# T4 of the last value pair grown by accumulating transfers, T1 of the first pair summed in DRAM

## The chip, the cores and the metric

The kernel runs on one core of a Trainium2 chip. The metric is the device time of one execution in microseconds; the median of three runs is taken. TensorE (PE in the profile) multiplies, VectorE (DVE), ScalarE (ACT) and GpSimd (POOL) work element by element, and the queues of SyncE (SP) and GpSimd issue transfers.

## What is computed

Two decoder layers on a sequence of 512 rows of 2048 numbers. Each layer has one input projection, three groups of attention heads, a gate, an output projection and a LayerNorm. Cut to what matters here:

```python
h = x @ w_in                    # 512 x 2048 by 2048 x 8278
fq, fk, fv, fg, ..., mq, mg = split(h)
y_fox = fox_attention(fq, fk, fv, ...) * silu(fg)
y_dsa = dsa_attention(dq, dk, dv, ...) * silu(dg)
y_mem = memory_attention(mq, mem @ w_mem_kv) * silu(mg)
x = layer_norm(ALPHA * x + concat(y_fox, y_dsa, y_mem) @ w_out)
```

The change touches the part of `x @ w_in` that the kernel calls the value columns: queries and keys of four heads, and the values and gates of twelve, 4096 columns in all.

## The kernel before, in words

**Numbers in two parts.** Each float32 operand is split into a high part (`whi`, by ScalarE, L217) and a low part (`wlo`, by VectorE, which subtracts the high part, L218). A product is three matmuls (L224 to L226): high by high, high by low, low by high. VectorE's `wlo` comes after ScalarE's `whi`, and TensorE needs both: the second matmul of a half already reads `wlo`.

**Seven products in place of eight.** The value columns come in four pairs of 512-column blocks (pair 0 to 3). For each pair the weights form a 2 by 2 grid of blocks, and the activations too, and the Strassen-Winograd scheme makes the result with seven products (`PRODUCTS`). Four of them read weight blocks as they lie in DRAM or a sum of blocks:

- P7 reads T3 = block (0,1) + block (1,1), summed in DRAM long before.
- Q6 reads T2 = T3 + block (0,0). The buffer that held T3 is grown: after it has been split for P7, GpSimd's queue issues a transfer that adds block (0,0) to it in place (`grow_w`, L283).
- Q4 reads T4 = T2 + block (1,0). VectorE adds the raw block (1,0), which was loaded for P2, to the buffer of T2 (`make_w`, L293). Until then the raw buffers of both are held.
- Q5 reads T1 = block (0,0) + block (0,1). SyncE loads one block into a raw buffer (L258) and the other into two slots (`other`, L264), and VectorE adds them (`pair_w`, L275).

**Order.** The order is written out by hand. A layer has the stages index, mem, values, heads and out, and a layer after the first begins with kv. In the stage values all pairs first run `VAL_FIRST` (P1, P7, P2, Q6 and Q4, mixed; its last chunks are Q6, Q6, P2, Q4, Q4), then all pairs run `VAL_SECOND` (Q5, Q5, Q3, Q3). So pair 3 of `VAL_FIRST` is followed by pair 0 of `VAL_SECOND`. Each name stands for two chunks (g = 0, 1). A chunk is 128 by 2048 numbers (1 MB) and is worked in two halves of 128 by 1024; a half feeds 12 matmuls of 512 columns. While half n is multiplied, half n+3 is split, half n+4 is summed by `pair_w`, and half n+2 starts to be grown. The split parts lie in four buffers each for `whi` and `wlo` (pool `whl`), so the split of half n+3 can only start once TensorE has left half n-1. The raw halves lie in six buffers (pool `raws`).

**What else VectorE does there.** In `VAL_FIRST` it builds the left operands S1 (for Q5) and S4 (for Q3) out of the activations (`val_operands`, L813, with the low parts in L823; the high parts are ScalarE's, L818), and it combines results on their way out of PSUM (`val_out`, L895 to L906). The results of Q5 and Q3 are copied out by ScalarE (L910). Q3 accumulates into the same two PSUM banks as Q5, so it can start only after that copy. The results go to DRAM by transfers on GpSimd's queue (`store_v`, L920 and L922).

**Sums in DRAM.** `all_sums` (L435) issues sums of weight blocks on GpSimd's queue: for each step of a sum a copy (L423) or an accumulating transfer (L404) of 1 MB from DRAM to DRAM. `paced` spreads the steps over the chunks, and outside the stage values each waits for a mark of VectorE (`pool_waits`, L391), so that GpSimd doesn't run ahead. In `weight_sums` T3 of the four value pairs of a layer takes 16 such transfers, which go out before that layer's values.

Of the kernel before, what the change touches and what calls it, by code (L numbers as in the profile page):

```python
# [80 lines left out]
PAIRS = 4  # L81
# [8 lines left out]
PAIRED = {"T1": ((0, 0), (0, 1))}  # L90
# [20 lines left out]
def all_chunks():  # L111

    out = []
    for l in range(DEPTH):
        out += [("mv", l, 0, g) for g in range(4)]
        out += [("mk", l, j, j * HD) for j in range(H_MEM)]
        out += layer_chunks(l)
    return out


def stream():

    wall = all_chunks()
    where = {c: i for i, c in enumerate(wall)}
    out = []

    def product(kind, l, name, pair, gs=(0, 1)):
        right = PRODUCTS[name][2]
        for g in gs:
            at = lambda step: where[kind, l, 2 * pair + step[1], 2 * step[0] + g]  # L130
            if kind == "val" and name in GROWN:
                of, step = GROWN[name]
                src = ("grown", (of, at(step)))
            elif kind == "val" and right in PAIRED:
                src = ("pair", tuple(at(step) for step in PAIRED[right]))
            elif isinstance(right, str):
                src = ("sum", (kind, l, right, pair, g))
            else:
                src = ("wall", at(right))
            out.append(({"val": "vs"}.get(kind, kind), l, (name, pair), g, src))  # L140

    for i, c in enumerate(wall):
        kind, l, j = c[:3]
        if kind == "out":
            if c == ("out", l, 0, 0):
                for name, pair in OUT_ORDER:
                    product("out", l, name, pair)
        elif kind == "val":
            if c == ("val", l, 0, 0):
                for order in (VAL_FIRST, VAL_SECOND):  # L150
                    for pair in range(PAIRS):
                        for name, g in order:
                            product("val", l, name, pair, (g,))
        else:
            out.append((*c, ("wall", i)))
    return out
# [20 lines left out]
def kernel(  # L177
# [25 lines left out]
    def uid(name):  # L203
        count[0] += 1
        return f"{name}_{count[0]}"
# [28 lines left out]
    for i, (kind, l, j, g, (how, key)) in enumerate(chunks):  # L234
        if how == "grown":
            of = place[kind, l, (key[0], j[1]), g]
            if j[0] == "Q6":
                grows[of] = i
            else:
                lender = place[kind, l, ("P2", j[1]), g]  # L240
                makes[max(of, lender)] = i
                lends[i] = (of, lender)
# [148 lines left out]
    def pool_waits():  # L391

        mark, seen = small("mark", 1), small("seen", 1)
        nc.vector.tensor_copy(mark, mhalf)  # L394
        nc.gpsimd.tensor_tensor(seen, mark, mhalf, op=ALU.mult)  # L395
# [4 lines left out]
    def block(kind, l, pair, g, step):  # L400
        return wall[where[kind, l, 2 * pair + step[1], 2 * step[0] + g]]

    def add_weights(key, src):
        nc.gpsimd.dma_start(sums[key], src, accum_op=ALU.add, max_dma_last_dim=4 * DM)  # L404

    def weight_sums(kind, l, names, pairs):

        for name in names:
            for n, step in enumerate(SUM_STEPS[name]):
                for pair in pairs:  # L410
                    for g in range(2):
                        key = (kind, l, name, pair, g)
                        if isinstance(step, str):
                            src = sums[kind, l, step, pair, g]
                        else:
                            src = block(kind, l, pair, g, step)
                        if now[1] != "values":
                            pool_waits()
                        if n:
                            add_weights(key, src)  # L420
                        else:
                            sums[key] = dram.tile([P, DM], F32, name=uid("sum"))
                            nc.gpsimd.dma_start(sums[key], src)  # L423
                        yield

    def paced(gen, steps=2):

        n = 0
        for _ in gen:
            n += 1  # L430
            while now[1] == "kv":
                yield 1
            yield {"mem": 1, "heads": 1, "out": 3, "index": 1 + now[0]}.get(now[1], steps)

    def all_sums():  # L435


        for l in range(DEPTH):
            yield from paced(weight_sums("val", l, ("T3",), range(PAIRS)))
            while now != (l, "heads"):  # L440
                yield 1
            yield from paced(weight_sums("out", l, ("T3", "T1", "T2", "T4"), range(2)))
# [659 lines left out]
    for i, (kind, l, j, col, _) in enumerate(chunks):  # L1102
        late = last_half(i)
        if kind == "out":
            step = OUT_ORDER.index(j)
            name, pair = j
# [11 lines left out]
        elif kind == "vs":  # L1118
            name, pair = j
# [151 lines left out]
        if kind == "small":  # L1271
            now = (l, "index")
            stored.clear()
            if l == 0:
                begin(all_sums(), whole=True)
# [136 lines left out]
```

## Time and profile before

| | us |
|---|---|
| median of 3 runs | 1935.13 (1933.09 to 1935.65) |
| the profiled execution | 1935.78 |
| its span, first to last instruction | 1933.6 |
| TensorE busy | 1907.8 |
| VectorE busy | 1462.4 |
| ScalarE busy | 970.4 |
| GpSimd busy | 323.5 |

The profiled execution takes 2.2 us more than its span. Times in the views are counted from the span's start. A busy span of TensorE is modelled, so that one matmul's time overlaps the next; how fast it goes is read from the distance between two starts. In brackets at the end of a row of the timeline stands the idle time of the engine before it, and what ended it.

### The profile page before, as it was taken

How to read it: one execution, taken by the hardware profiler on the slowest of the kernel's cores; microseconds unless marked ns; L12 is line 12 of the kernel's file. 1: busy time of each engine (PE TensorE's matmuls, PEld its weight loads, DVE VectorE, ACT ScalarE, POOL GpSimd, SP SyncE). 2: the span in 40 equal slices, each digit the busy share in tenths (PEclk: the TensorE clock that was granted, in tenths of full speed). 3: DMA queues.
4: the chain of work that ended last, by engine and by line, in shares of the span. 5: the costliest groups of instructions: out<-in, count | busy, mean ns of one | idle time of the engine just before them, and what ended most of it. 6: DMA issues, size and time to landing. Idle time of an engine off the chain costs nothing.

```text
span 1933.6 us, 26103 instructions
## 1 busy us (share of the span) xinstructions
PE 1907.8 (99%) x9282; PEld 1621.9 (84%) x9282; DVE 1462.4 (76%) x2407; ACT 970.4 (50%) x1538; POOL 323.5 (17%) x551
## 2 busy tenths in 40 slices
PE   9999999999999999999999999999989999999997
PEld 8998888887788888888899988888878888888886
DVE  6666667789876676688886877777898756677888
ACT  6564454444443545555474644544444445555453
POOL 0230001110123011210051200111111331112101
PEclk9999999999999999999999999999999999999999
DMA  9695247776998788998797934567779987789966
GB/s 363 236 282 165 77 111 204 206 207 210 338 304 231 237 237 240 263 328 305 255 289 205 260 113 154 141 176 200 207 249 332 298 236 234 240 240 266 343 197 152
DMA packets 148078, 451.08 MB, mean 233 GB/s; under 512 B 15456, under 2 KB 48224, under 8 KB 140780
## 3 DMA queue, kind: packets, MB, share of 16 engines
q1 hardware_dynamic: 117900, 283.70, 43.4%
q0 software_dynamic: 30048, 165.72, 33.4%
q8 instruction: 73, 1.20, 0.2%
q14 instruction: 57, 0.47, 0.1%
HBM read 411.58 MB, written 140.53 MB: 286 GB/s over the span
## 4 chain that ended last, share of the span: by engine, by line
PE 87%; DVE 8%; ACT 2%; issue 1%; DMA 0%; SPq 0%; POOL 0%; DVEq 0%; ACTq 0%; POOLq 0%
PE c L224 12%; PE c L226 12%; PE c L225 12%; PE v L224 10%; PE v L226 10%; PE v L225 10%; PE z L225 4%; PE z L226 4%; PE z L224 4%; DVE wlo L218 3%; PE pt L728 1%; DVE vx L813 1%; PE ix L646 1%; PE ix L645 1%; PE po L226 1%
## 5 line engine op out<-in xcount | busy, mean ns | idle before, releaser
L218 DVE TENSOR_TENSOR wlo<-raw,whi 128x1024 fp32r<-128x1024 f32 (+1 forms) x497 | 606.7, 1225 | 217.9 <-ACT whi L217 215.8
L217 ACT ACTIVATE whi<-raw 128x1024 fp32r<-128x1024 f32 (+1 forms) x497 | 521.9, 1054 | 363.6 <-PE v L226 228.7
L224 PE MATMUL c<-xh,whi 128*128 128x512 f32 (+1 forms) x1056 | 402.1, 381 | 0.0
L226 PE MATMUL c<-xh,wlo 128*128 128x512 f32 (+1 forms) x1056 | 398.3, 377 | 0.0
L225 PE MATMUL c<-xl,whi 128*128 128x512 f32 (+1 forms) x1056 | 397.3, 376 | 0.0
L226 PEld LDWEIGHTS c<-xh,wlo 128*128 128x128 f32 x1056 | 198.2, 188 | 32.4
L225 PEld LDWEIGHTS c<-xl,whi 128*128 128x128 f32 x1056 | 198.5, 188 | 30.4
L224 PEld LDWEIGHTS c<-xh,whi 128*128 128x128 f32 x1056 | 198.3, 188 | 30.0
L224 PE MATMUL v<-whi,vxh 128*128 128x512 f32 x512 | 201.5, 394 | 5.3 <-ACT vraw L910 5.3
L225 PE MATMUL v<-wlo,vxh 128*128 128x512 f32 x512 | 201.2, 393 | 3.6 <-DVE wlo L218 3.6
L226 PE MATMUL v<-whi,vxl 128*128 128x512 f32 x512 | 200.3, 391 | 0.0
L225 PE MATMUL z<-wlo,yh 128*128 128x512 f32 (+1 forms) x434 | 168.1, 387 | 2.5 <-DVE wlo L218 2.5
L224 PE MATMUL z<-whi,yh 128*128 128x512 f32 (+1 forms) x434 | 168.4, 388 | 0.0
L226 PE MATMUL z<-whi,yl 128*128 128x512 f32 (+1 forms) x434 | 167.8, 387 | 0.0
L225 PE MATMUL v<-wlo,xh 128*128 128x512 f32 x384 | 149.7, 390 | 1.1 <-DVE wlo L218 1.1
L224 PE MATMUL v<-whi,xh 128*128 128x512 f32 x384 | 149.4, 389 | 0.0
L226 PE MATMUL v<-whi,xl 128*128 128x512 f32 x384 | 149.4, 389 | 0.0
L395 POOL TENSOR_TENSOR seen<-mark,mhalf 128x1 f32<-128x1 f32 x96 | 25.9, 270 | 618.5 <-DVE mark L394 614.5
L225 PEld LDWEIGHTS v<-wlo,vxh 128*128 128x128 f32 x512 | 97.0, 189 | 26.5 <-DVE wlo L218 6.6
L224 PEld LDWEIGHTS v<-whi,vxh 128*128 128x128 f32 x512 | 96.9, 189 | 26.1 <-ACT vraw L910 6.1
L226 PEld LDWEIGHTS v<-whi,vxl 128*128 128x128 f32 x512 | 96.8, 189 | 20.1
L225 PEld LDWEIGHTS z<-wlo,yh 128*128 128x128 f32 x434 | 81.5, 188 | 20.2 <-DVE wlo L218 4.2
(222 smaller groups left out, 3085.0 us busy)
## 6 DMA issues: line engine op xcount, KB each, us to landing
raw<-in_wall_dram SPq DMA_DIRECT2D x338, 512.0 KB, 6.5
sum<-in_wall_dram POOLq DMA_DIRECT2D x48, 1024.0 KB, 11.2
raw<-sum SPq DMA_DIRECT2D x96, 512.0 KB, 5.8
v<-vraw POOLq DMA_DIRECT2D x96, 256.0 KB, 6.3
raw<-in_wall_dram POOLq DMA_DIRECT2D x32, 512.0 KB, 7.5
other<-in_wall_dram SPq DMA_DIRECT2D x64, 256.0 KB, 8.1
vraw<-v SPq DMA_DIRECT2D x64, 256.0 KB, 6.5
x<-z POOLq DMA_DIRECT2D x32, 256.0 KB, 5.1
```

The source lines that it names most:

```text
L217: nc.scalar.activation(hi, src, AF.Copy)
L218: nc.vector.tensor_tensor(lo, src, hi.bitcast(F32), op=ALU.subtract)
L224: nc.tensor.matmul(ps, ah, bh, start=start, stop=False, skip_group_check=more)
L225: nc.tensor.matmul(ps, ah, bl, start=False, stop=False, skip_group_check=more)
L226: nc.tensor.matmul(ps, al, bh, start=False, stop=stop, skip_group_check=more)
L395: nc.gpsimd.tensor_tensor(seen, mark, mhalf, op=ALU.mult)
L645: nc.tensor.matmul(o, st[:, qb * P:(qb + 1) * P], kh2[:, :w], start=True, stop=False)
L646: nc.tensor.matmul(o, st[:, qb * P:(qb + 1) * P], kl2[:, :w], start=False, stop=True)
L728: nc.tensor.transpose(tp[tb][:, toff + (qb - kt) * P:toff + (qb - kt + 1) * P], pr[b][:, off + kt * P:off + (kt + 1) * P], ident)
L813: nc.vector.tensor_tensor(d, acc, x, op=op)
```

## The change

For the last pair of a layer (pair 3), T4 is no longer added by VectorE: Q4 is entered in `grows`, as Q6 is, and the buffer of T2 is grown into T4 by an accumulating transfer of block (1,0) from DRAM on GpSimd's queue. For the first pair (pair 0), T1 is no longer loaded as two blocks and added by VectorE: it is summed in DRAM by `all_sums` after the T3 sums of the layer, and SyncE loads the sum. The other pairs stay as they were.

```diff
@@ stream
-            elif kind == "val" and right in PAIRED:
+            elif kind == "val" and right in PAIRED and pair > 0:
                 src = ("pair", tuple(at(step) for step in PAIRED[right]))
             elif isinstance(right, str):
                 src = ("sum", (kind, l, right, pair, g))
@@ tile_hybrid_kernel
         if how == "grown":
             of = place[kind, l, (key[0], j[1]), g]
-            if j[0] == "Q6":
+            if j[0] == "Q6" or j[1] == PAIRS - 1:
                 grows[of] = i
             else:
                 lender = place[kind, l, ("P2", j[1]), g]
@@ all_sums
         for l in range(DEPTH):
             yield from paced(weight_sums("val", l, ("T3",), range(PAIRS)))
+            yield from paced(weight_sums("val", l, ("T1",), (0,)))
             while now != (l, "heads"):
                 yield 1
```

The added line moves the lines behind it down by one, so L813 of before is L814 of after.

On VectorE, the first place is the splitting of Q6 of pair 3 in the first layer (`wlo` is its low part, `vx` a sum for S1, `acc` the scores of the top-key search). Before:

```order
L218 TENSOR_TENSOR wlo_4038<-raw_3892,whi_4037 128x1024
L293 TENSOR_TENSOR raw_3892<-raw_3892,raw_3981 128x1024
L676 MAX m_806_4058<-acc_1272 128x8
L677 MATCH_REPLACE acc_1272<-m_806_4058,acc_1272 128x384
L813 TENSOR_TENSOR vx_4061<-xh_450,vx_2292 128x256
L813 TENSOR_TENSOR vx_4061<-vx_4061,xl_451 128x256
L813 TENSOR_TENSOR vx_4061<-xh_454,vx_2292 128x256
L813 TENSOR_TENSOR vx_4061<-vx_4061,xl_455 128x256
L218 TENSOR_TENSOR wlo_4069<-raw_3894,whi_4068 128x1024
L293 TENSOR_TENSOR raw_3894<-raw_3894,raw_3983 128x1024
L218 TENSOR_TENSOR wlo_4089<-raw_3934,whi_4088 128x1024
```

The same place after:

```order
L218 TENSOR_TENSOR wlo_4060<-raw_3914,whi_4059 128x1024
L677 MAX m_816_4079<-acc_1272 128x8
L678 MATCH_REPLACE acc_1272<-m_816_4079,acc_1272 128x384
L814 TENSOR_TENSOR vx_4082<-xh_450,vx_2314 128x256
L814 TENSOR_TENSOR vx_4082<-vx_4082,xl_451 128x256
L814 TENSOR_TENSOR vx_4082<-xh_454,vx_2314 128x256
L814 TENSOR_TENSOR vx_4082<-vx_4082,xl_455 128x256
L218 TENSOR_TENSOR wlo_4091<-raw_3916,whi_4090 128x1024
L218 TENSOR_TENSOR wlo_4111<-raw_3956,whi_4110 128x1024
```

The add L293 behind each of Q6's four `wlo` is gone (two of the four are shown); nothing else on VectorE changes places there.

The second place on VectorE lies about forty instructions later, where Q4's last half and Q5's first are split and the first S4 sums are made. Before:

```order
L813 TENSOR_TENSOR vx_2292<-vx_2292,xl_618 128x256
L275 TENSOR_TENSOR raw_4251<-raw_4251,other_4253 128x512
L275 TENSOR_TENSOR raw_4251<-raw_4251,other_4255 128x512
L218 TENSOR_TENSOR wlo_4266<-raw_3936,whi_4265 128x1024
L823 TENSOR_TENSOR vxl_4225<-vx_4198,vxh_4224 128x512
L275 TENSOR_TENSOR raw_4257<-raw_4257,other_4259 128x512
L275 TENSOR_TENSOR raw_4257<-raw_4257,other_4261 128x512
L218 TENSOR_TENSOR wlo_4290<-raw_4251,whi_4289 128x1024
```

The same place after:

```order
L814 TENSOR_TENSOR vx_2314<-vx_2314,xl_618 128x256
L218 TENSOR_TENSOR wlo_4278<-raw_3958,whi_4277 128x1024
L824 TENSOR_TENSOR vxl_4247<-vx_4220,vxh_4246 128x512
L218 TENSOR_TENSOR wlo_4300<-raw_4273,whi_4299 128x1024
L814 TENSOR_TENSOR vx_2422<-xh_649,vx_2422 128x256
```

The adds L275 ahead of Q5's four `wlo` are gone, eight in a layer (four are shown). The raw halves `raw_4273` and so on now come from the sum in DRAM, and the eight loads of `other` are gone from SyncE's queue.

On GpSimd, the place is its queue around the growing of pair 3 in the first layer (`v` is the result in DRAM, `vraw` the tile that is stored). Before:

```order
L922 DMA v_166<-vraw_3556 128x512
L283 DMA raw_3892<-in_wall_dram 128x1024
L283 DMA raw_3894<-in_wall_dram 128x1024
L283 DMA raw_3934<-in_wall_dram 128x1024
L283 DMA raw_3936<-in_wall_dram 128x1024
L922 DMA v_169<-vraw_4192 128x512
```

The same place after:

```order
L923 DMA v_166<-vraw_3578 128x512
L283 DMA raw_3914<-in_wall_dram 128x1024
L283 DMA raw_3916<-in_wall_dram 128x1024
L283 DMA raw_3956<-in_wall_dram 128x1024
L283 DMA raw_3958<-in_wall_dram 128x1024
L283 DMA raw_3914<-in_wall_dram 128x1024
L283 DMA raw_3916<-in_wall_dram 128x1024
L283 DMA raw_3956<-in_wall_dram 128x1024
L283 DMA raw_3958<-in_wall_dram 128x1024
L923 DMA v_169<-vraw_4214 128x512
```

Each raw half is grown a second time, from T2 into T4, behind its first growing and ahead of the stores of pair 3's results. The new T1 sums stand elsewhere: in the first layer two copies and two accumulating transfers, each behind a mark of VectorE, directly behind the last T3 sum and the last rotary step of the index stage; in the second layer the same four between the stores of the residual rows, also behind the last T3 sum. TensorE's and ScalarE's instructions keep their order throughout.

## The prediction

> **What bounds the kernel now.** I begin with the page's line of busy times, which says whom the end waits for.
>
> ```profile
> PE 1907.8 (99%) x9282; PEld 1621.9 (84%) x9282; DVE 1462.4 (76%) x2407; ACT 970.4 (50%) x1538; POOL 323.5 (17%) x551
> ```
>
> TensorE is busy for 99% of the span, and the change takes nothing from it. What VectorE saves counts only where TensorE waits for VectorE, so the second view is TensorE's waits over the whole span.
>
> ```profile
> engine line waited for: us in total, times, longest us
> PE v L224 <- ACT vraw L910: 5.3, 2, 2.6
> PE v L225 <- DVE wlo L218: 5.1, 8, 0.9
> ```
>
> Both rows, by the `v`, belong to the value products. The third view, busy time by stretches of 10 us, shows where they lie (first layer, then second layer), and beside them four stretches that are needed below.
>
> ```profile
> core 0: us, PE busy (x) PEld busy (x) DVE busy (x) ACT busy (x) POOL busy (x), PEclk, DMA share, GB/s
> 440.00:450.00 10.00, 10.00 (x46) 8.29 (x45) 9.87 (x14) 5.30 (x6) 0.00 (x0) 1.00 0.25 87
> 480.00:490.00 10.00, 6.51 (x22) 4.66 (x21) 9.93 (x14) 6.02 (x8) 1.82 (x2) 0.85 0.95 318
> 1440.00:1450.00 10.00, 6.47 (x22) 4.76 (x21) 9.93 (x14) 6.00 (x8) 1.81 (x2) 0.83 0.95 316
> 140.00:160.00 20.00, 20.00 (x94) 16.74 (x93) 12.53 (x20) 10.28 (x21) 1.45 (x3) 1.00 1.04 255
> 160.00:200.00 40.00, 40.00 (x200) 34.01 (x199) 25.93 (x46) 18.89 (x46) 0.00 (x0) 1.00 0.33 117
> 1100.00:1120.00 20.00, 20.00 (x93) 16.73 (x92) 16.94 (x28) 10.88 (x22) 2.10 (x3) 1.00 0.69 229
> 1120.00:1140.00 20.00, 20.00 (x101) 16.91 (x100) 11.65 (x18) 9.99 (x24) 0.54 (x1) 1.00 0.24 80
> ```
>
> VectorE is full (9.9 of 10 us) where TensorE has gaps, and there the granted clock falls to 0.85 and 0.83. How much is lost in all is read from starts in TensorE's timeline.
>
> ```profile
> 453.30 0.39 PE L224 MATMUL v<-whi,xh 128*128 128x512 f32 x1
> ...
> 466.90 0.39 PE L224 MATMUL v<-whi,xh 128*128 128x512 f32 x1
> 467.88 0.50 PE L225 MATMUL v<-wlo,xh 128*128 128x512 f32 x1 [0.59 <-DVE wlo L218]
> ...
> 481.61 0.50 PE L225 MATMUL v<-wlo,vxh 128*128 128x512 f32 x1 [0.87 <-DVE wlo L218]
> ...
> 487.03 0.80 PE L224 MATMUL v<-whi,vxh 128*128 128x512 f32 x1 [2.62 <-ACT vraw L910]
> ...
> 490.77 0.40 PE L224 MATMUL v<-whi,vxh 128*128 128x512 f32 x1
> ...
> 1426.54 0.39 PE L224 MATMUL v<-whi,xh 128*128 128x512 f32 x1
> ...
> 1446.57 0.79 PE L224 MATMUL v<-whi,vxh 128*128 128x512 f32 x1 [2.63 <-ACT vraw L910]
> ...
> 1449.66 0.39 PE L225 MATMUL v<-wlo,vxh 128*128 128x512 f32 x1
> ```
>
> At 453.30 the last P2 chunk of pair 3 begins, at 466.90 the last half of Q4, at 487.03 Q3 of pair 0. From the first to the second lie five halves of 12 matmuls: 60 in 13.60 us, 0.227 us each. The next 60 take 20.13 us, so 6.53 us are lost. Behind the gap of 2.62 us the clock is halved: the nine matmuls from 487.03 to 490.77 take 3.74 us in place of 2.04, another 1.70. The first layer loses 8.2 us. In the second, 60 matmuls take 20.03 us and the seven behind the gap 3.09 in place of 1.59: 6.43 + 1.50 = 7.9 us. Together **16.1 us** is the most that can be won here.
>
> [...]
>
> Last, why VectorE is late: its timeline, and ScalarE's at the end of the stretch.
>
> ```profile
> 435.56 1.23 DVE L218 TENSOR_TENSOR wlo<-raw,whi 128x1024 fp32r<-128x1024 f32 x1 [1.49 <-ACT whi L217]
> ...
> 440.68 1.22 DVE L218 TENSOR_TENSOR wlo<-raw,whi 128x1024 fp32r<-128x1024 f32 x1
> ...
> 452.53 1.22 DVE L293 TENSOR_TENSOR raw<-raw,raw 128x1024 f32<-128x1024 f32 x1
> 453.67 0.68 DVE L823 TENSOR_TENSOR vxl<-vx,vxh 128x512 fp32r<-128x512 f32 x1
> ...
> 455.40 0.68 DVE L899 SCALAR_TENSOR_TENSOR vraw<-v,vraw 128x512 f32<-128x512 f32 x1
> ...
> 465.39 1.29 DVE L275 TENSOR_TENSOR raw<-raw,other 128x512 f32<-128x512 f32 x2
> 466.60 1.22 DVE L218 TENSOR_TENSOR wlo<-raw,whi 128x1024 fp32r<-128x1024 f32 x1
> ...
> 484.80 1.22 DVE L218 TENSOR_TENSOR wlo<-raw,whi 128x1024 fp32r<-128x1024 f32 x1
> ...
> 452.05 1.05 ACT L217 ACTIVATE whi<-raw 128x1024 fp32r<-128x1024 f32 x1
> ...
> 484.92 0.63 ACT L818 ACTIVATE vxh<-vx 128x512 fp32r<-128x512 f32 x1 [1.93 <-DVE vx L813]
> 485.45 1.04 ACT L217 ACTIVATE whi<-raw 128x1024 fp32r<-128x1024 f32 x1
> 486.40 1.06 ACT L910 ACTIVATE vraw<-v 128x512 f32<-128x512 f32 x2
> ```
>
> From 435.56 to 484.80 VectorE has no idle time; its last S4 sum ends at 484.80. ScalarE, in order, waits for that sum, and only then splits a half and copies Q5's bank (486.40), for which Q3 waits. So the 2.62 us put down to ScalarE are VectorE's as well.
>
> **The change part by part.** *The four L293 a layer.* The last one starts 1.14 us before the next instruction; four make 4.57 us. Not all of it comes through. L899 reads Q6's banks, and ahead of it on VectorE stands the `wlo` of Q4's first half, whose `whi` buffer comes free when TensorE leaves the half four earlier. That is 12 matmuls before 453.30, at 450.58. With 1.05 for `whi`, 1.14 for `wlo` and some 0.2 for hand-overs, L899 can start at about 452.9, against 455.40. So the bounds are 0 and 4.57; I take 2.5, and the other 2.1 become idle time.
>
> *The eight L275 a layer.* Two of them move the next instruction by 1.21 us (465.39 to 466.60): 4.84 us in all, every one in the unbroken chain behind L899, so I count them whole. VectorE's last S4 sum then ends 2.5 + 4.8 = 7.3 us earlier, at 477.5.
>
> *What is late next.* Without stalls Q3 is due at 466.90 + 13.60 = 480.50. From the end of the last sum to Q3's start it now takes 487.03 - 484.80 = 2.23 us, so the bank would be free at 479.7: 0.8 us to spare. The halves before have more: Q4's last half was 0.6 to 0.8 us late and gets 2.5 + 1.2 = 3.7; Q5's last half (481.61, due at 478.0) was 3.6 late and gets 7.3. So every stall of the stretch goes, and with the gap of 2.6 us the halved clock. The margin of 0.8 us is the thin place.
>
> *The new growing.* Four transfers a layer on GpSimd's queue. The rows are those of the present L283, and of GpSimd's first store of pair 3.
>
> ```profile
> L283 POOL DMA_DIRECT2D raw<-in_wall_dram x32: 851/866/904, 257.6 to 1389.0; - x32
> DMA to landing us min/median/max: 5.4/7.5/9.3
> 456.39 0.58 POOL L922 DMA_DIRECT2D v<-vraw  x1 [26.13 <-DVE vraw L899]
> ```
>
> GpSimd idles for 26 us just there, and the stores queued behind the new transfers wait for L899 anyway. The `wlo` of Q6's first half ends at 436.8; with 0.87 to issue and at worst 9.3 to land, T4 is there at 447.0, and ScalarE wants it at 450.58. The second half's `wlo` starts one L293 earlier than 440.68 and ends at about 440.8; T4 lands by 451.0 and is wanted at 453.30. The third and fourth have more. I take nothing. P2's raw halves come free at their split, so SyncE's loads start earlier; the share of the DMA engines is 0.25 there (440 to 450), so that costs nothing either.
>
> *T1 in DRAM.* Two copies and two accumulating transfers a layer, 4.2 MB, behind the T3 sums. At the 255 GB/s of the stretch from 140 to 160, which is full of such sums (share 1.04), that is an estimated 16.4 us of all DMA engines. The next 40 us of the first layer have two thirds free (26.8 us), and 1100 to 1140 of the second have 6.2 + 15.2 = 21.4 us. TensorE is busy throughout all four stretches, the full one too. So the cost lies between 0 and 16.4 us a layer; I take 0, by the row of the full stretch. GpSimd's eight marks are single-column instructions, and SyncE issues less. In the value stage 2 MB a layer are loaded in place of 4.
>
> *Sum.* 8.2 + 7.9 = 16.1 us off 1935.78 is 1919.7; the profiled execution lies 0.65 above the median, so the median goes to **1919.0 us**.
>
> **The rivals.** *Only T1's adds count.* If ScalarE's or TensorE's hand-overs swallow all of L293's gain (the bound 0), VectorE is 4.84 us earlier and Q3 1.7 us late. A gap of 1.7 us lies between 0.87, behind which no clock fell, and 2.62, behind which it did. So a layer wins 4.84 or 6.5 us, and the time is 1925.4 or 1922.1. For it speaks the thin margin, against it that L899 started 2.5 us behind its floor. Chance 0.15.
>
> *The growing lands late.* T4's first half is issued at 437.7 and wanted at 450.58, and TensorE feels it some 5.7 us after that, since a split stands three halves (8.2 us) ahead of its use and takes 2.4: it decides from a landing of 18.6 us. The sums from DRAM to DRAM show such times.
>
> ```profile
> L404 POOL DMA_DIRECT2D sum<-in_wall_dram x48: 805/823/928, 106.2 to 1769.9; - x48
> DMA to landing us min/median/max: 7.9/11.2/24.5
> ```
>
> At 24.5 us TensorE would lose 5.9 us and 1.7 of clock a layer, which gives back nearly all: 1934. Against it, the 32 present ones never took over 9.3. Chance 0.03.
>
> *The sums starve the weight loads* (slower). The transfers of SyncE and GpSimd in the stretch from 100 to 160, and SyncE's over the whole page:
>
> ```profile
> raw<-in_wall_dram SPq DMA_DIRECT2D x13, 512.0 KB, 17.5
> ...
> raw<-in_wall_dram SPq DMA_DIRECT2D x338, 512.0 KB, 6.5
> ```
>
> Beside the sums a weight half lands after 17.5 us in place of 6.5. A half of 24 matmuls takes 5.44 us there, and six raw buffers cover six of them, less some 2.5 for the split: it decides from about 30 us. If T1's four transfers carry the landing past that, TensorE pays at most their 16.4 us a layer, and the time is 1919.0 + 32.8 = 1951.8. [...] Chance 0.05.
>
> *The change does not reach the stall*: another user of VectorE's order holds ScalarE, and the time stays at 1935. The unbroken chain speaks against it. Chance 0.02.
>
> **How the numbers follow.** The forecast has 0.75. Its own range is 1917.0 to 1921.5: the runs of before lie within 2.6 us, and up to 1 us a layer may stay if the 0.8 us of margin is misjudged. With the first rival the range reaches to 1925.4 and holds 0.9. A measurement can tell about 0.2%, 3.9 us, from no change. Faster: 0.75 + 0.15 = 0.90. Within 0.2%: 0.03 + 0.02 = 0.05. Slower: 0.05.
>
> **What the profile after would show.** If right, TensorE's waits have no row with L911 (L910 of before) and at most a fraction of 5.1 us for `wlo` in `v`; 480 to 490 is full at clock 1.00 in both layers; VectorE has idle time of about 2 us ahead of L900 (L899 of before). If the growing is late, ScalarE's `whi` of Q4 waits for a transfer. If the loads starve, TensorE waits between 145 and 200. I am wrong if the waits for `wlo` or for Q5's copy stay in the same stretch though the adds are gone, or if they come back at pair 1, whose adds remain.

## The result, and the profile after

The changed kernel takes 1918.88 us (median of 4 runs, 1918.53 to 1919.13) against 1934.9 us before (1933.09 to 1935.65). The ratio is 0.9918, 95% interval 0.9901 to 0.9936: 16.0 us less. The profiled execution took 1919.06 us, its span is 1917.3 us.

TensorE's waits over the whole span, after:

```profile
engine line waited for: us in total, times, longest us
PE z L225 <- DVE wlo L218: 2.6, 4, 0.7
PE v L224 <- ACT memh L217: 1.5, 1, 1.5
PE warm L365 <- POOL mhalf L367: 1.4, 1, 1.4
PE lft L599 <- DVE lq L595: 0.2, 1, 0.2
PE v L225 <- DVE wlo L218: 0.2, 1, 0.2
```

The row with Q5's copy (5.3 us before) is gone, and the one for `wlo` in the value products fell from 5.1 to 0.2. The rows that are left lie outside the stretch; `memh` and `warm` are from the start of the kernel.

Busy time by stretches, after:

```profile
core 0: us, PE busy (x) PEld busy (x) DVE busy (x) ACT busy (x) POOL busy (x), PEclk, DMA share, GB/s
440.00:450.00 10.00, 10.00 (x46) 8.27 (x45) 8.56 (x14) 5.42 (x7) 2.59 (x3) 1.00 0.96 171
480.00:490.00 10.00, 10.00 (x46) 8.29 (x45) 8.13 (x12) 4.74 (x5) 1.78 (x2) 1.00 1.06 353
1440.00:1450.00 10.00, 10.00 (x46) 8.29 (x45) 8.19 (x13) 5.45 (x6) 1.70 (x2) 1.00 1.06 351
160.00:200.00 40.00, 40.00 (x199) 34.01 (x199) 25.84 (x47) 18.92 (x46) 2.38 (x5) 1.00 0.72 222
1100.00:1120.00 20.00, 20.00 (x99) 17.03 (x98) 15.53 (x26) 8.13 (x16) 3.57 (x6) 1.00 1.03 291
```

480 to 490 and 1440 to 1450 are full now, at clock 1.00. TensorE's timeline shows the last half of Q4 and the first matmul of Q3 of pair 0:

```profile
466.76 0.39 PE L224 MATMUL v<-whi,xh 128*128 128x512 f32 x1
...
480.36 0.39 PE L224 MATMUL v<-whi,vxh 128*128 128x512 f32 x1
```

The 60 matmuls between them take 13.60 us, where the kernel before took 20.13 us; in the second layer (1418.14 to 1431.74) it is 13.60 us again. The new transfers are seen in the share of the DMA engines: 0.96 from 440 to 450 (0.25 before), where T4 is grown, and 0.72 and 1.03 where the T1 sums run (0.33 and 0.69 before). TensorE is full beside them.

VectorE's timeline, and ScalarE's, at the places that the prediction computed:

```profile
446.34 1.23 DVE L218 TENSOR_TENSOR wlo<-raw,whi 128x1024 fp32r<-128x1024 f32 x1 [0.78 <-ACT whi L217]
...
451.78 1.23 DVE L218 TENSOR_TENSOR wlo<-raw,whi 128x1024 fp32r<-128x1024 f32 x1 [0.89 <-ACT whi L217]
452.92 0.68 DVE L900 SCALAR_TENSOR_TENSOR vraw<-v,vraw 128x512 f32<-128x512 f32 x1
...
477.44 1.22 DVE L218 TENSOR_TENSOR wlo<-raw,whi 128x1024 fp32r<-128x1024 f32 x1
...
477.55 0.63 ACT L819 ACTIVATE vxh<-vx 128x512 fp32r<-128x512 f32 x1 [1.32 <-DVE vx L814]
478.09 1.04 ACT L217 ACTIVATE whi<-raw 128x1024 fp32r<-128x1024 f32 x1
479.20 0.60 ACT L911 ACTIVATE vraw<-v 128x512 f32<-128x512 f32 x1
...
450.69 1.06 ACT L217 ACTIVATE whi<-raw 128x1024 fp32r<-128x1024 f32 x1 [0.86 <-PE v L226]
```

VectorE now waits for ScalarE's `whi` ahead of the instruction that reads Q6's banks (two of the three waits are shown; the third is 0.52 us), and ScalarE for TensorE, which still holds the buffer (last row). That instruction starts at 452.92, the last S4 sum ends at 477.44, and Q5's first bank is copied at 479.20, in time for Q3.

### The profile page after: what moved, and what is told of

Its sections match the earlier page's. It is cut to its first block, busy times and chain, and to the rows that moved or that the text cites. A ratio compares the mean times of both kernels' runs of the same rounds, so it can differ in the third digit from the quotient of the medians.

```text
span 1917.3 us, 26089 instructions
## 1 busy us (share of the span) xinstructions
PE 1900.6 (99%) x9282; PEld 1620.7 (85%) x9282; DVE 1444.0 (75%) x2391; ACT 970.8 (51%) x1538; POOL 340.3 (18%) x575
## 4 chain that ended last, share of the span: by engine, by line
PE 93%; DVE 4%; ACT 2%; issue 1%; DMA 0%; SPq 0%; POOL 0%; DVEq 0%; ACTq 0%; POOLq 0%
PE c L224 12%; PE c L226 12%; PE c L225 12%; PE v L226 11%; PE v L224 11%; PE v L225 11%; PE z L225 4%; PE z L226 4%; PE z L224 4%; PE pt L729 1%; PE ix L647 1%; PE ix L646 1%; PE po L226 1%; PE po L225 1%; PE po L224 1%
```

## The experiments

Theory A is that of the prediction: an unbroken chain on VectorE made TensorE wait. Theory B puts the gain into the transfers, and theory C counts every removed add whole. The names in brackets are those that the expectations use.

**VectorE's adds kept as idle work (adds_kept).** This tells VectorE's time apart from the transfers. All transfers are those of the changed kernel. Of VectorE's four adds for T4 in a layer, two stand behind the `wlo` of Q6's first chunk and two behind that of P2's last chunk, not all four behind Q6; the idle maxima stand in the same places.

```diff
+        if ... chunks[i][0] == "vs" and chunks[i][2] == ("Q5", 0):
+            for e in range(2):
+                d = raw[i][h][:, e * 512:(e + 1) * 512]
+                nc.vector.tensor_tensor(d, d, d, op=ALU.max)
...
+            if ... chunks[i][2:4] in ((("Q6", PAIRS - 1), 0), (("P2", PAIRS - 1), 1)):
+                nc.vector.tensor_tensor(r, r, r, op=ALU.max)
```

> The changed kernel, all its transfers included, but VectorE does an idle in-place maximum of the same size wherever before had an add of pair 3's T4 or pair 0's T1 (results unchanged). Theory A: VectorE's order and load are those of before, so the stalls are back whole: 1935 us, with a gap of 2.6 us ahead of Q3 in both layers. Theory B: the transfers are those of after, so 1919 us.

Measured: 1935.45 us (1932.96 to 1936.89), ratio to before 1.0003 (0.9994 to 1.0013). The whole gain is gone, and TensorE's waits are those of before (the edit moves L910 to L917):

```profile
PE v L225 <- DVE wlo L218: 5.3, 7, 0.9
PE v L224 <- ACT vraw L917: 5.3, 2, 2.6
```

Theory B falls: with all transfers of the change and VectorE's old load, nothing is won.

**T4 alone (t4_only).** Only the rule for `grows` is changed.

```diff
-            if j[0] == "Q6":
+            if j[0] == "Q6" or j[1] == PAIRS - 1:
```

> T4 of pair 3 is grown, T1 of pair 0 stays two loads and VectorE's adds. Theory A (VectorE's unbroken chain, L293 worth 2.5 us of 4.57 a layer because of its floor at 452.9): the last S4 sum ends 2.4 us earlier, at 482.4; Q3 of pair 0 is still 4.1 us late, its gap stays near 2.6 us and the clock is still halved once a layer: 1934.9 - 4.9 = 1930.0 us. Theory B (the gain is in the transfers, not in VectorE's time: raw buffers free earlier, fewer loads) gives the growing at most a part, with no link to VectorE's idle time. Theory C (each removed add counts whole): 4.57 us a layer, 1925.8 us.

Measured: 1928.2 us (1927.08 to 1929.9), ratio 0.9964 (0.995 to 0.9978), 6.4 us less, between A (4.9) and C (9.1). The waits and VectorE's timeline:

```profile
PE v L224 <- ACT vraw L910: 5.3, 2, 2.6
PE v L225 <- DVE wlo L218: 2.3, 4, 0.9
...
453.10 0.68 DVE L899 SCALAR_TENSOR_TENSOR vraw<-v,vraw 128x512 f32<-128x512 f32 x1
```

The instruction at Q6's banks starts at 453.10, as A has it, and the gap ahead of Q3 stays 2.6 us in both layers, as A has it. What A missed in the profiled execution is the clock: it was halved behind one of the two gaps only (below).

**T1 alone (t1_only).** The two T1 edits of the change, without that of `grows`.

```diff
-            elif kind == "val" and right in PAIRED:
+            elif kind == "val" and right in PAIRED and pair > 0:
...
+            yield from paced(weight_sums("val", l, ("T1",), (0,)))
```

> T1 of pair 0 is summed in DRAM, T4 of pair 3 stays VectorE's add. Theory A: 4.84 us a layer off the chain, Q3 is 1.7 us late in one gap; 1934.9 - 9.7 = 1925.2 us if that gap halves the clock as 2.6 us did, 1922 us if it doesn't. Theory C gives the same. Theory B (transfers): 8 MB of loads less in a full stretch, so nearly the whole 16 us, about 1919 us.

Measured: 1922.59 us (1921.41 to 1923.65), ratio 0.9937 (0.9922 to 0.9951). That is A without a halved clock, and the time of the prediction's first rival without the halved clock (1922.1). By the pages of before and after (512 KB halves from DRAM x338 and x330, sums x96 and x104, `other` of 256 KB x64 and x48) the loads fell by 4.2 MB in both layers together, not by the 8 MB of the expectation (and by half of that, not 4 MB, in the next experiment); theory B falls with either figure. TensorE's waits in the value products are one gap a layer:

```profile
PE v L224 <- ACT vraw L911: 2.9, 2, 1.5
```

**Half of T1 (t1_half).** The changed kernel, with the second chunk's T1 left to VectorE.

```diff
-            elif kind == "val" and right in PAIRED and pair > 0:
+            elif kind == "val" and right in PAIRED and (pair > 0 or g > 0):
```

> The changed kernel, but of T1 of pair 0 only the first chunk (g = 0) comes from the DRAM sum; the second keeps its two loads and four VectorE adds a layer, 2.42 us. Theory A: the last S4 sum ends 2.4 us later than 477.4, at 479.9, Q3 is 1.6 us late (0.8 us of margin used up first): 1918.9 + 3.2 = 1922.1 us without a halved clock, 1925 us with it. Theory B: 4 MB of loads more than the changed kernel, no stall to be named, 1919 to 1921 us.

Measured: 1921.97 us (1921.18 to 1922.64), ratio 0.9933 (0.9919 to 0.9948), with one gap of 1.5 us a layer where 1.6 was expected:

```profile
PE v L224 <- ACT vraw L911: 3.1, 2, 1.5
```

**Half of T4 (t4_second).** The changed kernel, with two of VectorE's four adds for T4 put back.

```diff
-            if j[0] == "Q6" or j[1] == PAIRS - 1:
+            if j[0] == "Q6" or (j[1] == PAIRS - 1 and g == 1):
```

> The changed kernel, but of pair 3's T4 only the second chunk (g = 1) is grown; VectorE keeps the two adds of the first chunk, 2.28 us a layer. Theory A (a floor at 452.9 for the instruction that reads Q6's banks, below which 2.1 us of the four adds were lost as idle time): the two adds that go are worth 2.28 us, the two that stay fit into the idle time; the instruction starts at 453.1, the last S4 sum ends 0.2 us later than in the changed kernel, within the 0.8 us of margin: 1919 us and no wait ahead of Q3. Theory C (each add counts whole): 2.28 us a layer back, less 0.8 of margin: 1922 us.

Measured: 1918.69 us (1918.0 to 1919.01), ratio 0.9915 (0.9899 to 0.9932), the same as the changed kernel, with half of its new growing. VectorE's timeline:

```profile
436.65 1.23 DVE L293 TENSOR_TENSOR raw<-raw,raw 128x1024 f32<-128x1024 f32 x1
441.76 1.23 DVE L293 TENSOR_TENSOR raw<-raw,raw 128x1024 f32<-128x1024 f32 x1
...
452.97 0.68 DVE L900 SCALAR_TENSOR_TENSOR vraw<-v,vraw 128x512 f32<-128x512 f32 x1
```

With two adds more, the instruction at Q6's banks starts 0.05 us later than in the changed kernel (452.92). The two fill what is idle time there. Theory C falls.

**One dose (dose_one).** The changed kernel with one pair of idle maxima ahead of Q5's last half.

```diff
+        if ... chunks[i][2:4] == (("Q5", 0), 1) and h == 1:
+            for e in range(2):
+                d = raw[i][h][:, e * 512:(e + 1) * 512]
+                nc.vector.tensor_tensor(d, d, d, op=ALU.max)
```

> The changed kernel with one idle pair of in-place maxima (1.21 us, results unchanged) on VectorE ahead of the last half of Q5 of pair 0. Theory A with a margin of 0.8 us: the last S4 sum ends 1.2 us later, Q3 is late by 0.4 us in both layers, so the waits show a row for Q5's copy of about 0.4 us twice, and about 1919.7 us. If the margin were larger than 1.2 us there would be no such row; if there were none, 1.2 us twice.

Measured: one execution, 1920.59 us. A single time can't tell half a microsecond; the row can (L911 is L915 here), and so can the starts in TensorE's timeline:

```profile
PE v L224 <- ACT vraw L915: 0.7, 2, 0.4
...
480.13 0.39 PE L226 MATMUL v<-whi,vxl 128*128 128x512 f32 x1
480.85 0.50 PE L224 MATMUL v<-whi,vxh 128*128 128x512 f32 x1 [0.34 <-ACT vraw L915]
```

The idle time in brackets counts from the modelled end of the matmul before. By the starts, Q3 comes 0.72 us behind the last matmul of Q5 in place of 0.23, so it is 0.49 us late, and the margin of the changed kernel is 1.21 less 0.49, about 0.7 us.

**T1 of all pairs in DRAM (t1_all).**

```diff
-            elif kind == "val" and right in PAIRED and pair > 0:
+            elif kind == "val" and right in PAIRED and pair >= PAIRS:
...
-            yield from paced(weight_sums("val", l, ("T1",), (0,)))
+            yield from paced(weight_sums("val", l, ("T1",), range(PAIRS)))
```

> The changed kernel with T1 of all four pairs summed in DRAM: twelve more transfers of 1 MB a layer among the sums, no L275 left on VectorE. Theory A: TensorE has nothing left to win in the value stage, and it is busy beside full DMA engines: 1919 us within 1. Rival (the sums starve the weight loads): the full stretch lasts some 50 us longer a layer, weight halves land past 30 us and TensorE waits between 145 and 260; at worst 12.6 MB at 255 GB/s, 49 us a layer, up to 2017 us.

Measured: 1920.05 us (1919.11 to 1920.41), ratio 0.9923 (0.9908 to 0.9938). The sums fill the DMA engines longer, and TensorE stays full:

```profile
160.00:200.00 40.00, 40.00 (x200) 34.03 (x199) 26.10 (x52) 18.90 (x46) 3.84 (x10) 1.00 0.94 328
200.00:240.00 40.00, 40.00 (x193) 33.60 (x192) 28.71 (x59) 18.28 (x36) 8.89 (x18) 1.00 0.91 213
```

Nothing starves, and nothing is won either: the other pairs' adds lie where TensorE doesn't wait. The median is 1.2 us above that of the changed kernel, a little more than was expected; what it is stays open.

**T4 grown in all pairs (t4_all).**

```diff
-            if j[0] == "Q6" or j[1] == PAIRS - 1:
+            if j[0] in ("Q6", "Q4"):
```

> The changed kernel with T4 grown by transfers in all four pairs, no L293 left on VectorE. Theory A: the adds of pairs 0 to 2 lie where TensorE doesn't wait, so nothing is won, and growing lands in time there too: 1919 us within 1. Rival (growing lands late): the first half of T4 would make ScalarE wait for a transfer in pairs 0 to 2, and TensorE behind it.

Measured: 1918.99 us (1918.68 to 1919.02), ratio 0.9918 (0.9903 to 0.9932), as the changed kernel. The 64 accumulating transfers land in time:

```profile
DMA to landing us min/median/max: 5.2/7.2/10.8
```

**The gap and the clock (before_a, before_b, gap_two).** Two more executions of the kernel before, and one of the changed kernel with five idle maxima a layer.

> The kernel before again, to see how often the gap of 2.6 us ahead of Q3 halves the clock (it did in both layers of the first profile, in one of two in t4_only and in one of two in adds_kept). [...]

> The same kernel once more, for two more gaps of 2.6 us: each with or without a halved clock, as above.

```diff
+        if ... chunks[i][0] == "vs" and chunks[i][2] == ("Q5", 0) and n % 4:
+            for e in range(2 if n % 4 > 1 else 1):
+                d = raw[i][h][:, e * 512:(e + 1) * 512]
+                nc.vector.tensor_tensor(d, d, d, op=ALU.max)
```

> The changed kernel with five idle in-place maxima of 512 columns (3.0 us a layer, results unchanged) on VectorE ahead of Q5 of pair 0. Theory A with 0.8 us of margin: Q3 is late by 2.2 us in one gap a layer. If the clock falls only behind gaps near 2.6 us and over: 1918.9 + 4.4 = 1923.3 us; with a halved clock in both layers 1926.5 us.

Measured: 1933.16 and 1933.12 us for the kernel before, 1926.96 us with five maxima. First TensorE's two gaps in before_a, and its stretches (the last columns are clock, DMA share and GB/s):

```profile
485.92 0.50 PE L224 MATMUL v<-whi,vxh 128*128 128x512 f32 x1 [2.58 <-ACT vraw L910]
1443.85 0.80 PE L224 MATMUL v<-whi,vxh 128*128 128x512 f32 x1 [2.63 <-ACT vraw L910]
...
470.00:495.00 25.00, 20.64 (x87) 15.75 (x87) 24.07 (x36) 11.43 (x14) 2.90 (x4) 1.00 0.85 265
1425.00:1455.00 30.00, 25.55 (x101) 19.51 (x100) 28.09 (x43) 13.02 (x15) 2.89 (x4) 0.94 0.88 290
```

The clock stays at 1.00 behind the gap of the first layer and is halved behind that of the second. It is so in before_b too. In t4_only both gaps last 2.63 us, and the clock is halved behind the first and not behind the second, as the distance of the next matmuls shows (0.43 us against 0.23):

```profile
484.63 0.80 PE L224 MATMUL v<-whi,vxh 128*128 128x512 f32 x1 [2.63 <-ACT vraw L910]
...
1441.82 0.50 PE L224 MATMUL v<-whi,vxh 128*128 128x512 f32 x1 [2.63 <-ACT vraw L910]
```

Then TensorE behind the second layer's gap with five maxima:

```profile
1437.89 0.50 PE L224 MATMUL v<-whi,vxh 128*128 128x512 f32 x1 [2.13 <-ACT vraw L915]
1438.23 0.39 PE L225 MATMUL v<-wlo,vxh 128*128 128x512 f32 x1
...
1439.39 0.58 PE L224 MATMUL v<-whi,vxh 128*128 128x512 f32 x1
1439.77 0.63 PE L225 MATMUL v<-wlo,vxh 128*128 128x512 f32 x1
...
1442.75 0.44 PE L226 MATMUL v<-whi,vxl 128*128 128x512 f32 x1
1443.03 0.39 PE L224 MATMUL v<-whi,vxh 128*128 128x512 f32 x1
```

Here a gap of 2.13 us sufficed, and the clock fell 1.5 us after TensorE had started again, for 3.4 us. Behind the first layer's gap of the same length it didn't fall. So the length of the gap doesn't decide alone; what else does was not shown. In this execution the mean clock was also lower in the kernel's first 20 us (0.91, against 1.00 in the changed kernel), where the edit changes nothing. With that and the one halved clock its time lies above the 1923.3 us of the gaps alone.

## Why the prediction was right, point by point

**The stall and its cause.** Shown. With VectorE's old load and the new transfers the time is 1935.45 us; each dose of VectorE's work on the chain brings back its gap ahead of Q3 (1.21 us of work: a gap of 0.35 us; 2.42 us: 1.5 us; all of it: 2.6 us and the waits before it).

**The adds of T4, 2.5 of 4.57 us.** Right. The floor was put at 452.9 and is 452.92. By then the changed kernel is 0.14 us ahead of the kernel before (its last P2 chunk begins at 453.16, not 453.30), so VectorE won 2.3 us there, where 2.5 was taken. The hand-overs ahead of it, put at some 0.2 us, were 0.28: TensorE leaves the half four earlier at 450.44 and `whi` starts at 450.69; `whi` ends at 451.75 and `wlo` starts at 451.78. The lost 2.1 us are the idle time of 0.52 + 0.78 + 0.89 = 2.2 us. Half of the growing does the same work, as t4_second shows.

**The adds of T1, counted whole.** Right: the last sum was put at 477.5 and ended at 477.44, or 477.58 with the same 0.14 us. Alone they leave a gap of 1.5 us (Q3 is 1.6 us late with the 0.15 us by which dose_one's starts exceed its idle time of 0.34), where 1.7 was worked out.

**The margin of 0.8 us.** Right within 0.1 us: about 0.7 by the dose.

**The growing at no cost.** Right. The 40 transfers landed in 5.5 to 8.7 us, within the 9.3 that was allowed:

```profile
436.93 0.86 POOL L283 DMA_DIRECT2D raw<-in_wall_dram  x1 [6.81 <-DVE wlo L218]
...
DMA to landing us min/median/max: 5.5/7.5/8.7
```

The first of T4's four is issued at 436.9, after GpSimd had been idle for 6.81 us. The trace shows no instruction that waited for one of the 40.

**The T1 sums at no cost.** Right, though they are felt: from 145 to 200, SyncE's weight halves land after 20.8 us at the median, where the kernel before had 5.7. Before and after, in this order:

```profile
raw<-in_wall_dram SPq DMA_DIRECT2D x8, 512.0 KB, 5.7
```

```profile
raw<-in_wall_dram SPq DMA_DIRECT2D x8, 512.0 KB, 20.8
```

That is still inside the 30 us that the prediction estimated as the point from which it would cost time. On GpSimd the first accumulating transfer of T1 waited 12.1 us for its copy to land, with nothing urgent behind it.

**The clock, 3.2 of the 16.1 us.** Right for the execution from which it was read, and too sure as a rule. In the two profiled executions, before and after, the spans differ by 1933.6 - 1917.3 = 16.3 us, and the two stretches account for 8.2 + 7.9 = 16.1 of them, since the changed kernel loses nothing there. But the working took the halved clock as certain behind a gap of 2.6 us, because both gaps of the one profile had it. Over five profiled executions with such gaps (before, before_a, before_b, t4_only, adds_kept) it came behind 6 of 10. So the mean loss by the clock was nearer 1.9 us than 3.2, and the sum nearer 14.9. Before_a and before_b, with one halved clock each, have spans 2.5 us shorter than the first profile: 1.6 us are the clock that wasn't halved in the first layer, the rest lies ahead of that gap, since Q3 starts behind it at 487.03 in the first profile, at 485.92 in before_a and at 485.65 in before_b. That the medians lie 16.0 us apart, as forecast from an execution with both clocks halved, is therefore in part luck; how often the clock was halved in the executions without a profile isn't known. The term fits t4_only too, whose expectation counted two halved clocks and whose profile shows one.

**The length of the gap.** The prediction had a gap of 2.6 us halve the clock, by two cases, and one of 0.87 us leave it. The runs show that gaps of 2.58 to 2.63 us (6 of 10) and of 2.13 us (1 of 2) can suffice and don't always. Behind the first layer's gap of 1.5 us in t1_only and in t1_half the clock stayed: from the copy of Q5's first bank to the third split behind it ScalarE took 6.45 and 6.46 us, where it took 8.05 in the kernel before with the halved clock. The halved stretch began up to 1.5 us behind the gap and was seen for 3.0 to 3.5 us. What decides beside the length was not shown.

**The rivals.** Only T1's adds count: it is the time of the T1 edits alone, 1922.59 us, and not that of the whole change. The growing lands late: no growing transfer took over 10.8 us, by the prediction's estimate 18.6 were needed. The sums starve the loads: not even with four times the T1 sums, where a weight half between 140 and 260 landed after 11.7 us at the median and TensorE waited for nothing from 100 to 300. The change doesn't reach the stall: it does.

## What to carry to other kernels

When one engine is in an unbroken chain behind the engine that sets the time, a removed instruction is worth its whole length only behind the last point where the chain must wait for someone else; ahead of it, part of the gain turns into idle time. Here the four adds of T4, 4.57 us a layer, won 2.3 us ahead of that point, and the adds of T1, 4.84 us behind it, won all. Find that floor in the timeline and cut behind it first: here two adds of T4 fewer did the work of four (1918.69 us against 1918.88). Such sums can be handed to transfers where nobody waits for them: here they cost nothing that the times show. It paid only where the chain held up the engine that sets the time; the same move in the other pairs won nothing (1920.05 and 1918.99 us). After such a cut, look how much margin the next late instruction has (here about 0.7 us), since what is added to the chain beyond that comes back as a stall: here 1.21 us of work made Q3 0.49 us late.

## What the runs showed of the hardware

- A gap on TensorE of 2.6 us halved its clock (0.50 from 487.1 to 490.1 in the kernel before) in 6 of 10 cases, one of 2.13 us in 1 of 2, one of 1.5 us in neither of the two cases in which its matmuls' pace can be read. The halved stretch was seen for 3.0 to 3.5 us and began up to 1.5 us after TensorE had resumed. Each such stretch cost 1.5 to 1.7 us, which added to the scatter of the time: before the change the first four runs lay within 2.6 us, after it within 0.6. The part ahead of the first layer's gap scattered as well: Q3 behind it started within 1.4 us among the three profiles of the kernel before.
- An in-place maximum of a tile with itself took VectorE the time of the add of two tiles (1.22 us each at 128x1024, 1.29 us each for a pair at 128x512, adds_kept against the kernel before): the stall of before came back to 0.2 us in the waits.
- Accumulating 512 KB from DRAM into SBUF landed after 7.5 us at the median with 32 and with 40 of them, after 7.2 with 64. With T1's DRAM sums queued beside them, plain loads of 512 KB took 20.8 us at the median between 145 and 200, against 5.7 in the kernel before.
